# Sums for the last small product on VectorE instead of DMAs, earlier loads and evenly spread splits, in a short convolution layer on one core

## The chip, the core and the metric

The kernel runs on one core of a Trainium2 chip. A core has engines that run on their own and wait for one another through semaphores: TensorE (PE in the profile; PEld is its weight loading) multiplies matrices into eight PSUM banks, VectorE (DVE), ScalarE (ACT) and GpSimd (POOL) work elementwise, and SyncE (SP) issues DMAs, which 16 DMA engines carry out. Each engine takes its own instructions in program order. POOL issues DMAs too, among them the accumulating ones, which add a source to what lies in DRAM. SP's DMAs and POOL's are told apart in the profile as queues q1 and q0.

The metric is the device time of one execution in microseconds. The time before is 778.96 us, the median of three runs (778.84 to 780.01).

## What is computed

With one layer (DEPTH = 1), only the short convolution mixer runs. All arrays are float32: 1024 positions, model width 1024, inner width CI = 2048.

```python
u = rms_norm(x, pre_norm)                              # (1024, 1024)
z, bg, cg, v = jnp.split(u @ w_in, 4, axis=-1)         # w_in: (1024, 4 * 2048)
y = bg * causal_dwconv(cg * v, conv_w) * jax.nn.silu(z)   # 3 taps, (1024, 2048)
m = y @ w_out                                          # w_out: (2048, 1024)
out = x + rms_norm(m, post_norm)
```

## The kernel before

**Matmuls.** A float32 operand is split into a high and a low part: ACT writes the high part (`hi`, rounded to PE's float32 type), and DVE writes the low part (`src - hi`). One product is then three matmuls: low by high, high by low, high by high. Such a pair, hi and lo, is called a piece here, and making it a split.

**First stage.** After the normalisation, `u @ w_in` is computed for 64 groups of 128 columns: four groups plainly, the other 60 in 20 triples of groups, each triple with 20 smaller products by a scheme that saves multiplications (line 931 on). Each triple has 20 steps `s`; behind each step's matmuls the program places reads of the banks, convolution, gates, splits of the next weights and DMAs, by hand. The gated results y go to DRAM as they come (`y_half`, L383): SP stores them into `y_d` and into sums `s_d` for the last stage, and POOL's accumulating DMAs (`more`, L371) finish these sums. Sums of blocks of w_out are made the same way in `t_d`.

**Last stage.** `y @ w_out` is done by products named a, d, b, c, e, f, g in this order (`OUT`, L853), again with sums of blocks as operands. Products a, b, c, e, g are large: two halves h, each 48 matmuls of 512 columns in four banks. Products d and f are small ones, done by seven products p in the order `FP = (1, 2, 6, 5, 7, 3, 4)`, each 24 matmuls of 256 columns (`small_mm`, L1003). Each small product needs one operand of w_out (u) and one of y (y), each of 512 KB. Operands 5, 6, 7 of both sides, 4 of u and 3 of y are sums of blocks. They are made in DRAM: `small_u` (L428) and `small_y` (L442) copy four blocks and then add to the copies with four accumulating DMAs. For d this happens during the triples, with the copies on SP's queue. For f's y the calls stand behind the halves of b and c (`SMALL_Y`, L1113 and L1131), and both copies and accumulates go out on POOL's queue.

**Order of the operands.** `PIECES` (L854) lists the 68 pieces in the order in which they are split, `FETCH` the loads. `fetch_unit` (L869) issues the next load on SP's queue: u's and the small operands into the six buffers of the pool `raw`, the large y operands (1 MB) into the pool `up`, whose 18 buffers also hold the pieces. `split_unit` (L898) makes the next piece: ACT's `hi` (L910, or L907 with the sign turned), DVE's `lo` (L911 or L908). `refill` (L894) issues loads as long as they are no more than five pieces ahead of the splits for small operands, two for large ones. The last triple (`t == END`) issues the first six loads, at the step s = 14 of the triple before and at its own steps 2, 8, 13, 15, 17 (L965), and splits eight pieces (L967). Behind the triples SP's program has the stores of the last gated tiles (L398, L399), then the load of `gpost` (L978), then the loads of `refill`.

**Around the products.** The loop at L1114 emits, for each half or small product, its matmuls and then a number of splits (`SPLITS`, L1110). What empties the banks stands between them: `combine` (L1094) for large products, and for small ones an ACT copy or a DVE sum per product (L1023 to L1029). A bank is used by several small products: 1, 6, 7 and 4 share one, 5 and 3 another. The third product of the order, 6, therefore waits until ACT or DVE has read product 1's result; 7 waits for 6's reading, 3 for 5's and 4 for 7's. These reads stand in ACT's and DVE's order among the splits. In the last lines each row block is normalised and stored (`finish_o`, L1058).

Of the kernel before, what the change touches and what calls it, by code (L numbers as in the profile page):

```python
# [8 lines left out]
F32 = mybir.dt.float32  # L9
# [11 lines left out]
def kernel(  # L21
# [11 lines left out]
    nc = tc.nc  # L33
    P = 128
    _, L, D = x.shape
# [31 lines left out]
    def flat(t):  # L67
        return t.rearrange("p a b -> p (a b)")
# [9 lines left out]
    s_d = dram.tile([P, 4, CH, HB], F32, tag="s_d", name="s_d")  # L78
    t_d = dram.tile([P, 4, CH, HB], F32, tag="t_d", name="t_d")
    SMALLS = "df"  # L80
    sm_y = {i: dram.tile([P, 4, CQ, FC], F32, tag=f"s{i}_d", name=f"s{i}_d") for i in SMALLS}
    sm_u = {i: dram.tile([P, 4, CQ, FC], F32, tag=f"t{i}_d", name=f"t{i}_d") for i in SMALLS}

    def rstd_start(ss, name, n=1):
# [37 lines left out]
    def new_u(name):  # L122
        return up.tile([P, 2, 2, HB], F32R, tag="u", name=name)
# [301 lines left out]
    def block_y(i, a, b):  # L425
        return quarter(s_d[:, SK[i]], b, a)

    def small_u(i, step, ks=slice(0, CQ)):  # L428
        t1, t2, t3, t4 = (sm_u[i][:, n, ks] for n in range(4))
        w11, w12, w21, w22 = (block_u(i, a, b)[:, ks] for a in (0, 1) for b in (0, 1))  # L430
        if step == 0:
            for dst, src in ((t1, w11), (t2, w11), (t3, w22), (t4, w21)):
                nc.sync.dma_start(dst, src)
        elif step == 1:
            more(t1, w12)
            more(t3, w12)
        elif step == 2:
            more(t2, t3)
        else:
            more(t4, t2)  # L440

    def small_y(i, step, ks=slice(0, CQ), queue=None):  # L442
        s1, s2, s3, s4 = (sm_y[i][:, n, ks] for n in range(4))
        y11, y12, y21, y22 = (block_y(i, a, b)[:, ks] for a in (0, 1) for b in (0, 1))
        if step == 0:
            for dst, src in ((s1, y21), (s2, y11), (s3, y21), (s4, y12)):
                (queue or nc.sync).dma_start(dst, src)
        elif step == 1:
            more(s1, y22)
            more(s3, y11)  # L450
        elif step == 2:
            more(s2, s1)
        else:
            more(s4, s2)
# [397 lines left out]
    FP = (1, 2, 6, 5, 7, 3, 4)  # L852
    OUT = [(i, h) for i in "adbcefg" for h in (FP if i in SMALLS else (0, 1))]  # L853
    PIECES, FETCH = [], []  # L854
    for i, h in OUT:
        for side in "uy":
            FETCH.append((side, i, h))
            PIECES += [(side, i, h, q) for q in ((0,) if i in SMALLS else (0, 1))]
    fetched, OP = [], {}

    def small_of(side, i, p):
        sums, blocks = (sm_u[i], block_u) if side == "u" else (sm_y[i], block_y)
        if p in (5, 6, 7):
            return sums[:, p - 5]
        if p == (4 if side == "u" else 3):
            return sums[:, 3]
        return blocks(i, *({1: (0, 0), 2: (1, 0), 3: (1, 1)} if side == "u" else {1: (0, 0), 2: (0, 1), 4: (1, 1)})[p])

    def fetch_unit():  # L869
        if not FETCH:  # L870
            return
        side, i, h = FETCH.pop(0)
        if i in SMALLS:
            t = raw.tile([P, CQ, FC], F32, tag="raw", name=f"r{side}_{i}{h}")
            nc.sync.dma_start(t, small_of(side, i, h))
            fetched.append(t)
            return
        js = slice(h * CQ, (h + 1) * CQ)
        far = slice(CH + h * CQ, CH + (h + 1) * CQ)
        if side == "u":  # L880
            plain_u = {"a": wov[:, js, :HB], "b": wov[:, far, :HB]}
            src = plain_u[i] if i in plain_u else t_d[:, TK[i], js]
            for q in (0, 1):
                r = raw.tile([P, 2, HB], F32, tag="raw", name=f"r{side}_{i}{h}{q}")
                nc.sync.dma_start(r, src[:, 2 * q : 2 * q + 2])
                fetched.append(r)
        else:
            plain_y = {"a": y_d[:, js, :HB], "b": y_d[:, far, :HB], "g": y_d[:, far, HB:]}
            src = plain_y[i] if i in plain_y else s_d[:, SK[i], js]
            t = up.tile([P, 2, 2, HB], F32, tag="u", name=f"r{side}_{i}{h}")  # L890
            nc.sync.dma_start(t.rearrange("p a b c -> p (a b) c"), src)
            fetched.extend([t[:, 0], t[:, 1]])

    def refill():  # L894
        while FETCH and len(fetched) <= len(OP) + (5 if FETCH[0][1] in SMALLS else 2):
            fetch_unit()

    def split_unit(delayed=False):  # L898
        n = len(OP)
        if n >= len(PIECES):  # L900
            return
        side, i, h, q = PIECES[n]
        t = new_u(f"o{side}_{i}{h}{q}")
        src, hi, lo = flat(fetched[n]), flat(t[:, 0]), flat(t[:, 1])
        turn = h == 6 if i in SMALLS else (i == "c") != (h == 1)
        if side == "u" and turn:
            nc.scalar.mul(hi, src, -1.0)  # L907
            low = lambda: nc.vector.scalar_tensor_tensor(lo, src, -1.0, hi.bitcast(F32), op0=ALU.mult, op1=ALU.subtract)  # L908
        else:
            nc.scalar.copy(hi, src)  # L910
            low = lambda: nc.vector.tensor_sub(lo, src, hi.bitcast(F32))  # L911
        if delayed:
            low_us.append(low)
        else:
            low()
        OP[side, i, h, q] = t
# [14 lines left out]
    for t in range(len(TRIPLES)):  # L931
        for s, i in enumerate(ORDER if t else ORDER_0, 1):
            now[0] += 1
            product(t, i)
            read(t, i)
            run_lows()
            while low_us:
                low_us.pop(0)()
            if t == 0:
                first_chunk(s)  # L940
                if s in LOWS:
                    low_u(LOWS[s][0], kks=LOWS[s][1])
            run_due()
            for unit in (SPLIT if t else SPLIT_0).get(s, ""):
                split_w(t, unit)
            if t == 0 and s in HIGHS:
                high_u(HIGHS[s])
            for unit in (NEXT if t else NEXT_0).get(s, ""):
                split_w(t + 1, unit)
            sums(t + 1, (SUMS if t or s > 15 else SUMS_0).get(s, ()))  # L950
            if s == 14:
                fetch_triple(t + 2)
            if s in (7, 14, 20):
                run_later()
            if 2 <= t < 2 + 2 * CH:
                j = (t - 2) // 2
                if t % 2 == 0 and s == 3:
                    fetch_t(j)
                if t % 2 == 0 and s == 15:
                    add_t(j, 0)  # L960
                if t % 2 == 1 and s in (15, 20):
                    add_t(j, 1 + (s == 20))
            for do, *of_small in EARLY.get((t, s), ()):
                do(*of_small)
            if t == END - 1 and s == 14 or t == END and s in (2, 8, 13, 15, 17):  # L965
                fetch_unit()
            if t == END and s in (6, 9, 11, 13, 15, 17, 19, 20):  # L967
                split_unit(True)
# [138 lines left out]
        else:  # L1107
            norm_square(q + TH, 0)

    SPLITS = {("a", 0): 5, ("a", 1): 5, ("c", 0): 5, ("c", 1): 5, ("e", 0): 6, ("e", 1): 5}  # L1110
    SPLITS.update({(i, p): 2 for i in SMALLS for p in FP})
    SPLITS.update({("d", 3): 1, ("d", 4): 1, ("f", 7): 1, ("f", 3): 0, ("f", 4): 0})
    SMALL_Y = {("b", 0): 0, ("b", 1): 1, ("c", 0): 2, ("c", 1): 3}  # L1113
    for n, (i, h) in enumerate(OUT[:-2]):  # L1114
        if (i, h) == ("f", FP[0]):
            load_res(0)
            load_res(1)
        splits = SPLITS.get((i, h), 4)
        if i in SMALLS:
            small_mm(i, h)  # L1120
        for q in range(1 if i in SMALLS else TH):
            if i not in SMALLS:
                out_mm(i, h, q)
                if h == 1 and q > 0:
                    combine(i, q - 1)
            for z in range(splits if i in SMALLS else (splits + TH - 1 - q) // TH):
                split_unit()
                refill()
        if i not in SMALLS and h == 1:
            combine(i, TH - 1)  # L1130
        if (i, h) in SMALL_Y:  # L1131
            small_y("f", SMALL_Y[i, h], queue=nc.gpsimd)
        if i == "c":
            early_half(2 * h)
            early_half(2 * h + 1)
        if i == "f" and h in FP[:TH]:
            early_half(FP.index(h) + TH)
        if i == "f" and h in (3, 4):
            for q in (0, 1) if h == 3 else (2, 3):
                norm_square(q, 1)  # L1140
                finish_o(q)
        if i == "f" and h == 7:
            for t in range(2, NT):
                load_res(t)
# [33 lines left out]
```

## Time and profile before

| | |
|---|---|
| median of 3 runs | 778.96 us (778.84 to 780.01) |
| the profiled execution, its own time | 777.1 us |
| its span, first to last instruction | 775.3 us |
| mean granted TensorE clock | 0.993 |
| last triple's end, first matmul of a | 606.66 us |
| d's matmuls | 628.42 to 660.32 us |
| f's first matmul | 725.6 us |
| g's first matmul | 746.60 us |

Times inside the profile count from the span's start. In a row of a timeline stand start, duration, engine, line, operation, out<-in by the program's names (buffer numbers left out) and, in brackets, the engine's idle time just before and what released it. `ru_d` and `ry_d` are loaded operands of d, `ou_d` and `oy_d` the pieces made of them, `pd` d's banks, `gx` and `res` what its banks are read into; `sd_d` and `sf_d` are the sums of y for d and f in DRAM. "SPq" is SP issuing a DMA, "DMA a<-b" a transfer on its way.

### The profile page before, as it was taken

To read this page: it belongs to the slowest core of one execution; us is meant where nothing else is said; L and a number is where in the kernel's file an instruction comes from. 1 tells how busy PE (TensorE), PEld (TensorE's weight loads), DVE (VectorE), ACT (ScalarE), POOL (GpSimd) and SP (SyncE) were. 2 spreads that over 40 slices of the span, in tenths; PEclk is the share of its full clock that TensorE was granted. 3 is DMA by queue.
4 is the path that set the end of the run, shared out by engine and by line. 5 is a ranking of instruction groups with operands and counts; after the bars stand their busy time and mean duration, and the time that the engine had idled before them with its cause. 6 is when DMAs were issued, how large, how long until landed. Compare 5 with 4: busy or idle time off the path is not lost.

```text
span 775.3 us, 10514 instructions
## 1 busy us (share of the span) xinstructions
PE 758.3 (98%) x3530; PEld 635.0 (82%) x3530; DVE 509.9 (66%) x774; ACT 467.5 (60%) x897; POOL 496.9 (64%) x604
## 2 busy tenths in 40 slices
PE   9999999999999999999999999999999986999996
PEld 8888888888888888888888888888888876888985
DVE  6898776465657565664655565666567755668887
ACT  8869756556656665655666465647548364546742
POOL 0678978778887977797898988889962321100012
PEclk9999999999999999999999999999999998999999
DMA  9402347459377458466877877795659499994944
GB/s 338 125 1 69 96 113 179 125 113 252 70 195 163 116 146 201 105 164 150 188 179 171 188 159 192 147 248 114 148 110 281 94 362 358 354 324 163 376 168 164
DMA packets 123975, 139.67 MB, mean 180 GB/s; under 512 B 6104, under 2 KB 89360, under 8 KB 123408
## 3 DMA queue, kind: packets, MB, share of 16 engines
q1 hardware_dynamic: 107136, 111.72, 44.2%
q0 software_dynamic: 16768, 27.27, 22.1%
q8 instruction: 28, 0.46, 0.2%
q14 instruction: 27, 0.22, 0.1%
q10 hardware_dynamic: 16, 0.00, 0.0%
HBM read 120.09 MB, written 60.82 MB: 233 GB/s over the span
## 4 chain that ended last, share of the span: by engine, by line
PE 88%; DVE 4%; DMA 4%; issue 1%; ACT 1%; POOL 0%; SPq 0%; DVEq 0%; ACTq 0%
PE pX L136 8%; PE pX L137 8%; PE pX L138 8%; PE pY L136 7%; PE pY L137 7%; PE pY L138 7%; PE pV L137 4%; PE pV L138 4%; PE pV L136 4%; PE pW L137 2%; PE pZ L137 2%; PE pW L138 2%; PE pZ L138 2%; PE pW L136 2%; PE pZ L136 2%; DMA ry_b<-y_d 2%
## 5 line engine op out<-in xcount | busy, mean ns | idle before, releaser
L366 DVE TENSOR_TENSOR sn<-sn,pY 128x512 f32<-128x512 f32 x57 | 39.2, 687 | 56.3 <-PE pY L138 26.8
L342 POOL TENSOR_TENSOR g<-g,sn 128x512 f32<-128x512 f32 x29 | 40.2, 1392 | 34.8 <-ACT sn L340 28.3
L366 DVE TENSOR_TENSOR sn<-sn,pX 128x512 f32<-128x512 f32 x57 | 39.3, 689 | 33.5 <-PE pX L138 33.5
L340 ACT ACTIVATE sn<-sn 128x512 f32<-128x512 f32 x24 | 15.2, 633 | 64.1 <-DVE sn L366 40.1
L1070 POOL TENSOR_TENSOR res<-xr,res 128x512 f32<-128x512 f32 x4 | 6.6, 1648 | 72.2 <-DVE res L1069 72.2
L360 ACT ACTIVATE sn<-pV 128x512 f32<-128x512 f32 x38 | 20.6, 596 | 48.0 <-PE pV L138 48.0
L315 POOL TENSOR_TENSOR g<-sn,g 128x512 f32<-128x512 f32 x23 | 31.0, 1349 | 28.6 <-DVE sn L364 28.6
L358 ACT COPY sn<-pZ 128x512 f32<-128x512 f32 x19 | 11.2, 589 | 46.7 <-PE pZ L138 46.7
L372 POOL DMA_DIRECT2D s_d<-s_d x24 | 22.9, 954 | 20.8 <-DMA s_d<-y_d 14.0
L324 POOL TENSOR_TENSOR g<-g,sn 128x512 f32<-128x512 f32 x20 | 28.3, 1413 | 11.7 <-DVE sn L366 11.3
L182 POOL TENSOR_TENSOR raw<-raw 128x256 f32<-128x256 f32 x40 | 32.3, 919 | 0.0
L187 POOL TENSOR_TENSOR raw<-e,raw 128x256 f32<-128x256 f32 x40 | 31.1, 858 | 1.3
L364 DVE TENSOR_TENSOR g<-pY,g 128x512 f32<-128x512 f32 x15 | 10.4, 692 | 30.7 <-PE pY L138 30.7
L183 POOL TENSOR_TENSOR e<-raw,raw 128x512 f32<-128x512 f32 x20 | 26.2, 1312 | 1.6
L1014 PE MATMUL pd<-ou_d,oy_d 128*128 128x256 f32 x56 | 17.2, 308 | 8.7 <-ACT gx L1023 7.4
L136 PE MATMUL pp<-b,wn 128*128 128x512 f32 x62 | 24.6, 397 | 0.0
L137 PE MATMUL pp<-b,wn 128*128 128x512 f32 x62 | 24.4, 393 | 0.0
L138 PE MATMUL pp<-b,wn 128*128 128x512 f32 x62 | 24.2, 390 | 0.0
L305 DVE SCALAR_TENSOR_TENSOR g<-g,cw,cv 128x512 f32<-128x512 f32 x30 | 22.5, 749 | 1.7
L237 DVE TENSOR_TENSOR wE<-wE,wE 128x512 fp32r<-128x512 f32 x20 | 13.7, 687 | 14.0 <-ACT wE L236 14.0
L305 DVE SCALAR_TENSOR_TENSOR cv<-g,cw,cv 128x512 f32<-128x512 f32 x30 | 22.4, 748 | 0.0
L189 POOL TENSOR_TENSOR e<-raw 128x256 f32<-128x256 f32 x20 | 21.8, 1088 | 0.0
(418 smaller groups left out, 3040.9 us busy)
## 6 DMA issues: line engine op xcount, KB each, us to landing
raw<-in_sc_w_in SPq DMA_DIRECT2D x64, 512.0 KB, 5.3
t_d<-in_sc_w_out SPq DMA_DIRECT2D x32, 256.0 KB, 4.5
s_d<-g SPq DMA_DIRECT2D x29, 256.0 KB, 2.1
s_d<-s_d POOLq DMA_DIRECT2D x24, 256.0 KB, 4.6
y_d<-g SPq DMA_DIRECT2D x23, 256.0 KB, 2.7
t_d<-in_sc_w_out POOLq DMA_DIRECT2D x16, 256.0 KB, 7.8
t_d<-t_d POOLq DMA_DIRECT2D x16, 256.0 KB, 4.7
xr<-in_x SPq DMA_DIRECT2D x8, 512.0 KB, 7.8
```

Source lines behind the costliest of these rows:

```text
L136: nc.tensor.matmul(ps, lo, u[:, 0, kk], start=first, stop=False, skip_group_check=True)
L137: nc.tensor.matmul(ps, hi, u[:, 1, kk], start=False, stop=False, skip_group_check=True)
L138: nc.tensor.matmul(ps, hi, u[:, 0, kk], start=False, stop=last, skip_group_check=True)
L182: 0: lambda: (add(w2[:, 0], w2[:, 0], w2[:, 1]), add(w2[:, 2], w2[:, 1], w2[:, 2])),
L183: 1: lambda: sub(e[:, 0:2], w2[:, 0::2], w0[:, 0::2]),
L187: 5: lambda: (sub(w0[:, 2], e[:, 3], w0[:, 2]), sub(w0[:, 0], e[:, 3], w0[:, 0])),
L305: nc.vector.scalar_tensor_tensor(g if j == TAPS - 1 else ps, g, tap(c, j), ps, op0=ALU.mult, op1=ALU.add)
L315: nc.gpsimd.tensor_mul(g, src, g)
L324: nc.gpsimd.tensor_mul(cv, cv, src)
L342: when([(c, "cv", h), (c, "silu", h)], (c, "z", h), {"cv": 1, "silu": 1}, lambda: nc.gpsimd.tensor_mul(cv_of(c, h), cv_of(c, h), t))
L366: nc.vector.tensor_sub(a, a, ps)
L372: nc.gpsimd.dma_start(dst, src, accum_op=ALU.add)
```

## The change

Four things change in the last stage.

1. The four copies and four accumulating DMAs that made f's sums of y in DRAM are gone, and with them the buffer `sf_d`. SP loads the four blocks of y that f needs ("Y" entries), and DVE adds them in SBUF: sum 5 from two blocks, sum 6 from sum 5 and a block, sum 7 from two blocks, sum 3 from sum 6 and a block. The sums lie in `xr` (5 and 6) and in the third part of `res`, `C22` (3 and 7), both of which are used otherwise only later. Operands 1, 2 and 4 are split from the blocks themselves.
2. f's pieces are ordered anew: first its seven y pieces, with 5 ahead of 6 and 7, then its seven u pieces. Sums 5 and 7 are added at their own split, sum 6 at the split of 5, and sum 3 at the split of 6.
3. The last triple issues two loads more, at its steps 18 and 20: operand 2 of d, of both sides.
4. `SPLITS` gives b 5 and 5 (it was the default, 4 and 4), and e 5 and 4 (it was 6 and 5). The total stays the same.

`fetched` becomes a table by piece number, since loads and pieces no longer come in the same order.

```diff
-    sm_y = {i: dram.tile([P, 4, CQ, FC], F32, tag=f"s{i}_d", name=f"s{i}_d") for i in SMALLS}
+    sm_y = {"d": dram.tile([P, 4, CQ, FC], F32, tag="sd_d", name="sd_d")}
...
-    for i, h in OUT:
-        for side in "uy":
-            FETCH.append((side, i, h))
-            PIECES += [(side, i, h, q) for q in ((0,) if i in SMALLS else (0, 1))]
-    fetched, OP = [], {}
+    for i in "adbcefg":
+        if i == "f":
+            n = len(PIECES)
+            FETCH += [("Y", "f", (0, 0), n), ("Y", "f", (1, 0), n + 1), ("Y", "f", (1, 1), n + 1), ("Y", "f", (0, 1), n + 2)]
+            PIECES += [("y", "f", p, 0) for p in (1, 5, 6, 7, 2, 3, 4)]
+            for p in FP:
+                FETCH.append(("u", "f", p, len(PIECES)))
+                PIECES.append(("u", "f", p, 0))
+            continue
+        for h in FP if i in SMALLS else (0, 1):
+            for side in "uy":
+                FETCH.append((side, i, h, len(PIECES)))
+                PIECES += [(side, i, h, q) for q in ((0,) if i in SMALLS else (0, 1))]
+    fetched, OP, blocks_f = {}, {}, {}
...
-            nc.sync.dma_start(t, small_of(side, i, h))
-            fetched.append(t)
+            nc.sync.dma_start(t, block_y(i, *h) if side == "Y" else small_of(side, i, h))
+            if side == "Y":
+                blocks_f[h] = flat(t)
+            else:
+                fetched[n] = flat(t)
...
-        while FETCH and len(fetched) <= len(OP) + (5 if FETCH[0][1] in SMALLS else 2):
+        while FETCH and FETCH[0][3] <= len(OP) + (5 if FETCH[0][1] in SMALLS else 2):
             fetch_unit()
+
+    sum_f = {}
+
+    def sum_of_f(p):
+        if p not in sum_f:
+            a, b = {
+                5: lambda: (blocks_f[1, 0], blocks_f[1, 1]),
+                6: lambda: (sum_of_f(5)[1], blocks_f[0, 0]),
+                7: lambda: (blocks_f[0, 0], blocks_f[1, 0]),
+                3: lambda: (sum_of_f(6)[1], blocks_f[0, 1]),
+            }[p]()
+            t = new_u(f"oy_f{p}0")
+            sum_f[p] = t, {5: xr[:, 0], 6: xr[:, 1], 3: flat(C22[:, :2]), 7: flat(C22[:, 2:])}[p]
+            nc.vector.tensor_add(sum_f[p][1], a, b)
+        return sum_f[p]
...
-        t = new_u(f"o{side}_{i}{h}{q}")
-        src, hi, lo = flat(fetched[n]), flat(t[:, 0]), flat(t[:, 1])
+        if (side, i) == ("y", "f") and h in (3, 5, 6, 7):
+            t, src = sum_of_f(h)
+            if h in (5, 6):
+                sum_of_f({5: 6, 6: 3}[h])
+        else:
+            t = new_u(f"o{side}_{i}{h}{q}")
+            src = blocks_f[{1: (0, 0), 2: (0, 1), 4: (1, 1)}[h]] if (side, i) == ("y", "f") else fetched.pop(n)
+        hi, lo = flat(t[:, 0]), flat(t[:, 1])
...
-            if t == END - 1 and s == 14 or t == END and s in (2, 8, 13, 15, 17):
+            if t == END - 1 and s == 14 or t == END and s in (2, 8, 13, 15, 17, 18, 20):
                 fetch_unit()
...
-    SPLITS = {("a", 0): 5, ("a", 1): 5, ("c", 0): 5, ("c", 1): 5, ("e", 0): 6, ("e", 1): 5}
+    SPLITS = {("a", 0): 5, ("a", 1): 5, ("b", 0): 5, ("b", 1): 5, ("c", 0): 5, ("c", 1): 5, ("e", 0): 5, ("e", 1): 4}
...
-    SMALL_Y = {("b", 0): 0, ("b", 1): 1, ("c", 0): 2, ("c", 1): 3}
...
-        if (i, h) in SMALL_Y:
-            small_y("f", SMALL_Y[i, h], queue=nc.gpsimd)
```

More of the change, by code (lines that the diff above doesn't have):

```diff
@@ L426, in block_y, with small_u @@
         return quarter(s_d[:, SK[i]], b, a)
-    def small_u(i, step, ks=slice(0, CQ)):
+    def small_u(i, step, ks):
         t1, t2, t3, t4 = (sm_u[i][:, n, ks] for n in range(4))
@@ L440, in small_u, with small_y @@
             more(t4, t2)
-    def small_y(i, step, ks=slice(0, CQ), queue=None):
+    def small_y(i, step, ks):
         s1, s2, s3, s4 = (sm_y[i][:, n, ks] for n in range(4))
@@ L446, in small_y @@
             for dst, src in ((s1, y21), (s2, y11), (s3, y21), (s4, y12)):
-                (queue or nc.sync).dma_start(dst, src)
+                nc.sync.dma_start(dst, src)
         elif step == 1:
@@ L871, in fetch_unit @@
             return
-        side, i, h = FETCH.pop(0)
+        side, i, h, n = FETCH.pop(0)
         if i in SMALLS:
-            t = raw.tile([P, CQ, FC], F32, tag="raw", name=f"r{side}_{i}{h}")
-            nc.sync.dma_start(t, small_of(side, i, h))
-            fetched.append(t)
+            t = raw.tile([P, CQ, FC], F32, tag="raw", name=f"r{side}_{i}{h if side != 'Y' else h[0] * 2 + h[1]}")
+            nc.sync.dma_start(t, block_y(i, *h) if side == "Y" else small_of(side, i, h))
[3 more added lines that the diff above has]
+                fetched[n] = flat(t)
             return
@@ L885, in fetch_unit @@
                 nc.sync.dma_start(r, src[:, 2 * q : 2 * q + 2])
-                fetched.append(r)
+                fetched[n + q] = flat(r)
         else:
@@ L891, in fetch_unit @@
             nc.sync.dma_start(t.rearrange("p a b c -> p (a b) c"), src)
-            fetched.extend([t[:, 0], t[:, 1]])
+            fetched[n], fetched[n + 1] = flat(t[:, 0]), flat(t[:, 1])
     def refill():
-        while FETCH and len(fetched) <= len(OP) + (5 if FETCH[0][1] in SMALLS else 2):
+        while FETCH and FETCH[0][3] <= len(OP) + (5 if FETCH[0][1] in SMALLS else 2):
             fetch_unit()
+    sum_f = {}
[11 more added lines that the diff above has]
+        return sum_f[p]
     def split_unit(delayed=False):
```

## The prediction

> **What bounds the kernel now.** I read the page first, then the stretches of the last stage, then what TensorE (PE) waited for there.
>
> ```profile
> span 775.3 us, 10514 instructions
> PE 758.3 (98%) x3530; PEld 635.0 (82%) x3530; DVE 509.9 (66%) x774; ACT 467.5 (60%) x897; POOL 496.9 (64%) x604
> ```
>
> PE is busy for 98% of the span, so only its 17 us of idle time, or the tail, can be won without taking matmuls away. The stretches show where the idle time lies (columns: busy time of PE, PEld, DVE, ACT, POOL; granted clock; DMA share; GB/s):
>
> ```profile
> core 0: us, PE busy (x) PEld busy (x) DVE busy (x) ACT busy (x) POOL busy (x), PEclk, DMA share, GB/s
> 630.00:640.00 10.00, 7.40 (x62) 7.19 (x61) 7.82 (x7) 9.04 (x12) 3.13 (x4) 1.00 1.06 366
> 640.00:650.00 10.00, 6.08 (x49) 5.67 (x47) 4.41 (x5) 3.09 (x4) 1.15 (x2) 0.94 1.05 373
> 650.00:660.00 10.00, 7.79 (x46) 7.58 (x47) 6.90 (x7) 5.05 (x6) 0.89 (x1) 0.72 1.10 342
> 660.00:670.00 10.00, 10.00 (x47) 8.34 (x47) 7.29 (x8) 7.45 (x8) 2.13 (x2) 1.00 1.06 389
> ```
>
> From 630 to 660 PE loses 8.7 us, the DMA engines are full, and the clock falls to 0.72 behind the longest pause. What PE waited for from 616 us on (us in total, times, longest):
>
> ```profile
> PE pd L1014 <- ACT gx L1023: 7.4, 2, 4.8
> PE pd L1014 <- DVE gx L1027: 1.1, 1, 1.1
> PE pf L1014 <- DVE res L1027: 0.4, 1, 0.4
> PE pd L1014 <- ACT gx L1025: 0.2, 1, 0.2
> ```
>
> All but 0.4 us is product d. PE's timeline gives its size (the starts of d's first and second small product, and of b):
>
> ```profile
> 628.42 0.28 PE L1014 MATMUL pd<-ou_d,oy_d 128*128 128x256 f32 x1
> ...
> 631.29 0.28 PE L1014 MATMUL pd<-ou_d,oy_d 128*128 128x256 f32 x1
> ...
> 660.32 0.40 PE L996 MATMUL po_b<-ou_b,oy_b 128*128 128x512 f32 x1
> ```
>
> A small product takes 631.29 - 628.42 = 2.87 us, so d's seven need 20.1 us. They took 660.32 - 628.42 = 31.9: **11.8 us are lost in d**, pauses and slow clock together. That is the most this change can win there.
>
> Why ACT and DVE are late is in the chain that ended last (start, us, what):
>
> ```profile
> 617.58 7.11 DMA ry_d<-s_d
> 624.76 1.06 ACT oy_d L910
> 625.85 1.24 DVE oy_d L911
> 627.11 7.68 DMA ry_d<-sd_d
> ...
> 635.95 1.24 DVE oy_d L911
> ...
> 637.63 15.60 DMA ry_b<-y_d
> 653.25 1.05 ACT oy_b L910
> ...
> 656.69 0.61 DVE gx L1027
> ```
>
> PE waits for an emptied bank; the copy or sum that empties it (L1023, L1027) stands in ACT's and DVE's order behind splits, and the splits wait for loads. The loads go round through six raw buffers: load, split, next load, about 9.5 us a round (617.58 to 627.11). The last link is ry_b, 1 MB, 15.6 us on its way. From its landing at 653.23 to b's start at 660.32 are 7.1 us of splits, bank reading and one small product, so b starts 7.1 us after ry_b lands, or when d's matmuls are through, whichever is later. SP issued nothing for 19 us before that:
>
> ```profile
> 595.54 0.36 SPq L875 DMA_DIRECT2D ry_d<-s_d  x1
> 615.12 0.33 SPq L398 DMA_DIRECT2D s_d<-g  x1
> ```
>
> It stood at the store of the last gated tile. And POOL's queue, which has nothing else to do, sends f's sums of y into the same stretch:
>
> ```profile
> 635.72 2.50 POOL L447 DMA_DIRECT2D sf_d<-s_d  x3
> 645.82 0.75 POOL L447 DMA_DIRECT2D sf_d<-s_d  x1 [7.59 <-issue]
> 649.60 1.29 POOL L372 DMA_DIRECT2D sf_d<-s_d  x1 [3.04 <-issue]
> ```
>
> In the program they stand behind b's halves, but POOL waits only for their data, so they collide with the loads of d and b. The DMA queues (packets, MB, share of the 16 engines) for 617 to 636 us, and then for 636 to 654:
>
> ```profile
> q1 hardware_dynamic: 2894, 5.96, 89.5%
> ```
>
> ```profile
> q1 hardware_dynamic: 2386, 4.47, 67.0%
> q0 software_dynamic: 720, 2.36, 37.4%
> ```
>
> q1 carries SP's transfers, q0 POOL's. In the second stretch q0 takes 0.374 x 18.0 = 6.7 us of the engines' time. A megabyte of q1 costs 0.895 x 19.0 / 5.96 = 2.85 us in the first and 0.67 x 18.0 / 4.47 = 2.70 us in the second.
>
> **The change part by part.**
>
> *f's sums off the DMA queues.* Four copies and four accumulates of 512 KB go, and SP loads four blocks for f where it loaded seven operands. POOL's accumulates of s_d stay:
>
> ```profile
> s_d<-s_d POOLq DMA_DIRECT2D x24, 256.0 KB, 4.6
> ```
>
> One of them, 0.26 of the 2.36 MB, goes out in 636 to 654 (POOL's last, just before its three copies), so 6.7 x 2.10 / 2.36 = 6.0 us of engine time come free ahead of ry_b's landing. The ends: nothing, if the loads wait for raw buffers and not for the engines; all 6.7 if the accumulate costs little. I take 6.0, since the engines stand at 1.05 of full and 15.6 us for 1 MB is no buffer's wait: ry_b was issued long before. What goes after 654 us is hidden, as PE is full from 660.
>
> The Trainium skill, page "DMA: Bandwidth & Descriptors", section "Anatomy of one DMA", prices a GpSimd transfer at 2.0 us plus its bytes by 436 GB/s; by that the 2.10 MB hold the engines for 4.8 us and the next item's 1 MB for 2.4, and the sum below would be an estimate of 7.2, not 8.7. The row, 6.7 us for 2.36 MB, is dearer per byte than the page.
>
> *Two more operands of d in the last triple.* ru_d2 and ry_d2 are issued at the triple's steps 18 and 20, ahead of the store at which SP stood, with raw buffers free (a's first pieces are split by then). So 1 MB leaves the queue that starts at 617: 2.7 us by q1's price. SP issues two DMAs more while it had nothing to do: no cost. The wait goes to ru_d6, two operands further on. The ends: 0, if the buffers alone limit, and 3.2 us, a third of a 9.5 us round for two of six buffers. I take 2.7.
>
> *What is late next.* Sum: ry_b lands 6.0 + 2.7 = 8.7 us earlier, near 644.5, and b starts 8.7 us earlier, as this stays below the 11.8 us at which d's matmuls would set it. A second count agrees: d7's operands are now issued at about 618 to 620 instead of near 627, are split near 632 to 633, ry_b's issue follows near 633.5, and the 2 MB ahead of it with its own 1 MB, at 2.7 us each, end at 641.6 if nothing else is in the way. Of the 11.8 us some 3 stay, before d's last product, which waits for the bank that L1027 empties behind b's first low halves.
>
> *Four additions on DVE.* They fall in c's second half; c, e and f slide forward with b. Their kind is the low half of a split, and two such in a row and DVE's later stretches read:
>
> ```profile
> 707.00 1.23 DVE L911 TENSOR_TENSOR ou_f<-ru_f,ou_f 128x1024 fp32r<-128x1024 f32 x1 [0.19 <-ACT ou_f L910]
> 708.14 1.22 DVE L911 TENSOR_TENSOR oy_f<-ry_f,oy_f 128x1024 fp32r<-128x1024 f32 x1
> ```
>
> ```profile
> 697.00:718.20 21.20, 21.20 (x95) 17.54 (x95) 16.69 (x19) 13.78 (x20) 0.00 (x0) 1.00 0.51 173
> 730.00:740.00 10.00, 10.00 (x85) 9.97 (x84) 10.00 (x16) 7.51 (x12) 0.00 (x0) 1.00 0.95 371
> ```
>
> One costs 1.14 us of DVE's time, four 4.6. The even spread (b 5 and 5, e 5 and 4) puts two splits ahead of c's second half, so that 697 to 718 holds two instructions more than before: 2.3 us. The sum for operand 7 is made just when it is needed, so its low half waits for ACT's copy, about 1.1 us. That is 3.4 us against 21.20 - 16.69 = 4.5 us of idle DVE. I cost it at **nothing**: that idle time hides it. Without the cover it costs one for one, because in f, from 730 to 740, DVE is full (10.00 of 10.00) and PE reads its banks again only when DVE has emptied them. The added waits: ACT's copies of the sums wait for DVE, and behind them stand c's reads of its banks, which nothing on PE needs before g. The sums lie in buffers (xr, C22) whose next writers come half a product later. Raw buffers are held longer by the four blocks; f's u operands behind them are still asked for five pieces ahead of their splits. Nothing.
>
> *Sum.* 8.7 us off a span of 775.3 gives 766.6, and off the profiled execution's own 777.1 us, 768.4. The median shown, 778.96, lies 1.9 us above that execution; the same gain makes it **770.3 us**.
>
> **The rivals.**
>
> *Less relief.* If the buffers' round and not the engines set the pace, only the earlier issue helps, or part of q0's time goes to loads that are not yet needed, since SP issues c's right behind b's. Gain 2.7 to 6: 773 to 776.3. For it: the chain goes through splits as well as loads. Against: ry_b's 15.6 us. 0.20.
>
> *All of it.* If the two queues shared evenly while both had work, q0 cost up to half of 636 to 654, 9.0 us; with 2.7 that is 11.7, d's matmuls set b's start, and the time is about 767. The rows speak against: 37.4% against 67.0%. The Trainium skill, same page, section "Queues, rings and completion order", states such a turn by turn sharing. 0.14.
>
> *DVE keeps f.* The additions cost more than the idle time, and f's start is 1 to 4 us late: 771.3 to 774.3. Against it: 3.4 against 4.5 us. 0.06.
>
> *Slower.* The blocks come too late. DVE goes in order, so an addition that waits for its block holds every split behind it, all of e's and f's. It needs them near 697 - 8.7 = 688 us. The first 4.5 us are idle time, each further one is lost, and from 13.2 us late on the gain is eaten. A load that goes out only when needed, at ry_b's 15.6 us, would cost 2.4 us: 781. Against it: the blocks are asked for half a product before they are needed, and the DMA share near there is 0.51. 0.04.
>
> *Nothing.* The waits in d move to another load with no gain: 777.4 to 780.5. 0.04.
>
> **How the numbers follow.** The forecast, 768.8 to 773, has 0.52. The range goes from all of d's loss won and f's 0.4 us too, 766.6, to the earlier issue alone, 776.3; it leaves out the last two cases. A measurement here can tell about 0.2%, 1.6 us, from no change. Faster by more: 0.52 + 0.20 + 0.14 + 0.06 = 0.92. Within: 0.04. Slower: 0.04.
>
> **What would show it.** Right: ru_d2 and ry_d2 issued near 596 to 606 us; no sf_d transfer; q0's share in 636 to 654 near 5%; ry_b on its way for 9 to 11 us and landed near 644.5; b's first matmul near 651.6; no clock below 0.9 there; PE full from b to f. Wrong: ry_b landing after 650 (less relief); a pause of PE above 1 us in f (DVE); DVE waiting for a block load in c.

## The result, and the profile after

The changed kernel takes **771.16 us** (median of 4 runs, 770.88 to 771.81), the kernel before in the same comparison 778.9 us. The ratio is 0.9904 with a 95% interval of 0.9885 to 0.9922: faster by 7.7 us, where 8.7 were forecast (770.3 us). Compared once more beside the last experiments, it took 770.06 us against 778.67, 0.9892 (0.9878 to 0.9905). The forecast lies between the two medians. What the profiles show of the 1.1 us between them comes below.

The profiled execution is the slowest of the first four, 771.81 us. The head of its page, two of its stretches (columns as before: busy time of PE, PEld, DVE, ACT, POOL; granted clock; DMA share; GB/s), and then what PE waited for from 616 us on (us in total, times, longest). The changed file's lines are L1047 to L1049 for `small_mm` (L1014 to L1016 before), L1029 for `out_mm` (L996), L1056 and L1060 for the copy and the sum out of d's banks (L1023, L1027), L943 and L944 for the two halves of a split (L910, L911), L922 for the new additions:

```profile
span 769.9 us, 10498 instructions
PE 757.7 (98%) x3530; PEld 633.9 (82%) x3530; DVE 513.3 (67%) x778; ACT 466.2 (61%) x897; POOL 489.3 (64%) x596
```

```profile
640.00:650.00 10.00, 6.83 (x55) 6.42 (x54) 6.01 (x7) 6.47 (x7) 0.00 (x0) 1.00 1.06 386
650.00:660.00 10.00, 10.00 (x49) 8.93 (x49) 7.99 (x8) 6.86 (x8) 0.00 (x0) 0.83 1.02 423
```

```profile
PE pd L1047 <- DVE gx L1060: 1.9, 1, 1.9
PE pd L1047 <- ACT gx L1056: 1.2, 1, 1.2
PE pf L1047 <- DVE res L1060: 0.4, 1, 0.4
```

PE's waits in d have shrunk from 8.7 us to 3.1. The DMA engines are as full as before; but the queues of 636 to 654 us show other freight (packets, MB, share of 16 engines):

```profile
q1 hardware_dynamic: 2988, 6.84, 97.1%
q0 software_dynamic: 144, 0.26, 7.9%
```

SP's loads move 6.84 MB where they moved 4.47, and POOL's queue falls from 2.36 MB to 0.26. SP issues the two added operands of d at 596.50 and 597.27, 18 us ahead of the store at which it stands:

```profile
596.50 0.46 SPq L884 DMA_DIRECT2D ru_d<-t_d  x1
597.27 0.36 SPq L884 DMA_DIRECT2D ry_d<-s_d  x1
```

The chain of waits from ry_b to d's last small product, and below it PE's timeline of that product and of b's start:

```profile
634.60 11.09 DMA ry_b<-y_d
...
645.71 1.05 ACT oy_b L943
...
646.79 0.99 DVE oy_b L944
...
647.93 0.80 DVE oy_b L944
...
649.07 0.70 DVE gx L1060
```

```profile
649.80 0.39 PE L1047 MATMUL pd<-ou_d,oy_d 128*128 128x256 f32 x1 [1.95 <-DVE gx L1060]
...
651.10 0.28 PE L1048 MATMUL pd<-ou_d,oy_d 128*128 128x256 f32 x1
651.22 0.36 PE L1049 MATMUL pd<-ou_d,oy_d 128*128 128x256 f32 x1
651.39 0.42 PE L1047 MATMUL pd<-ou_d,oy_d 128*128 128x256 f32 x1
651.60 0.42 PE L1048 MATMUL pd<-ou_d,oy_d 128*128 128x256 f32 x1
...
653.95 0.63 PE L1029 MATMUL po_b<-ou_b,oy_b 128*128 128x512 f32 x1
```

ry_b lands at 645.69 (653.23 before). The order on DVE is the old one: two low halves of oy_b, and behind them the sum `gx` that empties the bank of d's last product. New is what the matmuls' starts show. Up to 651.10 they follow 0.12 us apart; from 651.39 on, 0.21. The clock has fallen (0.83 in the stretch from 650 to 660), 1.6 us after PE took up work again, and d's last product takes 653.95 - 649.80 = 4.15 us in place of 2.87.

In the kernel before, the same slow clock stood one product earlier:

```profile
651.08 0.58 PE L1014 MATMUL pd<-ou_d,oy_d 128*128 128x256 f32 x1 [4.80 <-ACT gx L1023]
651.46 0.42 PE L1015 MATMUL pd<-ou_d,oy_d 128*128 128x256 f32 x1
651.68 0.42 PE L1016 MATMUL pd<-ou_d,oy_d 128*128 128x256 f32 x1
...
657.35 0.39 PE L1014 MATMUL pd<-ou_d,oy_d 128*128 128x256 f32 x1 [1.13 <-DVE gx L1027]
```

There the slow product was followed by another 1.13 us of waiting for DVE, so its slowness cost nothing; the last product ran from 657.35 to 660.32, its matmuls 0.12 us apart again. That is why the slow matmuls, which went on to 655.5, added nothing to the 7.1 us from ry_b's landing to b's start.

### The profile page after: what moved, and what is told of

Read it like the earlier page. It is cut to its first block, busy times and chain, and to the rows that moved or that the text cites. A ratio compares the mean times of both kernels' runs of the same rounds, so it can differ in the third digit from the quotient of the medians.

```text
span 769.9 us, 10498 instructions
## 1 busy us (share of the span) xinstructions
PE 757.7 (98%) x3530; PEld 633.9 (82%) x3530; DVE 513.3 (67%) x778; ACT 466.2 (61%) x897; POOL 489.3 (64%) x596
## 4 chain that ended last, share of the span: by engine, by line
PE 94%; DMA 2%; DVE 2%; issue 1%; ACT 0%; SPq 0%; DVEq 0%
PE pX L136 8%; PE pX L138 8%; PE pX L137 8%; PE pY L136 7%; PE pY L138 7%; PE pY L137 7%; PE pV L138 4%; PE pV L137 4%; PE pV L136 4%; PE po_x L1031 3%; PE po_x L1029 3%; PE po_x L1030 3%; PE pW L138 2%; PE pZ L138 2%; PE pW L136 2%; PE pZ L136 2%
## 5 line engine op out<-in xcount | busy, mean ns | idle before, releaser
L340 ACT ACTIVATE sn<-sn 128x512 f32<-128x512 f32 x24 | 15.2, 631 | 64.1 <-DVE sn L366 40.1
L237 DVE TENSOR_TENSOR wC<-wC,wC 128x512 fp32r<-128x512 f32 x20 | 13.8, 688 | 11.9 <-ACT wC L232 11.9
```

The lines of the kernel that those rows point to most:

```text
L237: lows.append(lambda: nc.vector.tensor_sub(x[:, 1], ps, x[:, 0].bitcast(F32)))
```

## The experiments

Twelve kernels were run in three groups, each group beside the kernel before on one chip. Its medians there are 777.43 us (early operands, sums alone, old spread, copies back on POOL), 778.29 (additions three times, four early, filler, splits behind) and 778.67 (the others). Stage a starts between 606.66 and 607.57 us in the profiles, so events are compared as distances. "To ry_b" is the time from a's first matmul to ACT's first split of ry_b, which starts 0.02 us after the landing; "to b" goes on from there to b's first matmul.

| kernel | median us | ratio to before (95%) | to ry_b | to b |
|---|---|---|---|---|
| before | 777.4 to 778.9 | 1 | 46.6 | 7.07 |
| changed | 771.16 | 0.9904 (0.9885 to 0.9922) | 38.5 | 8.24 |
| changed, again | 770.06 | 0.9892 (0.9878 to 0.9905) | 37.7 | 7.08 |
| early operands alone | 775.69 | 0.9976 (0.9966 to 0.9986) | 42.7 | 9.38 |
| sums on DVE without early operands | 772.02 | 0.9933 (0.992 to 0.9947) | 40.1 | 7.07 |
| changed, old spread of splits | 771.47 | 0.9925 (0.9913 to 0.9938) | 38.0 | 8.37 |
| changed, f's copies back on POOL | 775.89 | 0.9972 (0.9959 to 0.9984) | 43.3 | 8.65 |
| before, f's copies by SP in order | 771.39 | 0.9909 (0.9894 to 0.9924) | 40.3 | 7.08 |
| changed, additions three times | 776.47 | 0.9976 (0.9966 to 0.9986) | 38.6 | 8.32 |
| changed, four operands early | 768.5 | 0.9877 (0.9859 to 0.9895) | 36.6 | 7.07 |
| changed, filler matmuls | 770.03 | 0.9901 (0.9885 to 0.9916) | 38.0 | 7.07 |
| before, b's splits behind | 772.85 | 0.9932 (0.992 to 0.9945) | 46.8 | 2.36 |
| changed, b's splits behind | 766.23 | 0.9849 (0.9834 to 0.9864) | 37.8 | 4.17 |
| the same, four operands early | 766.57 | 0.9847 (0.9834 to 0.9861) | 36.7 | 5.18 |

### Which part of the change wins what

Early operands alone, on the kernel before:

```diff
-            if t == END - 1 and s == 14 or t == END and s in (2, 8, 13, 15, 17):
+            if t == END - 1 and s == 14 or t == END and s in (2, 8, 13, 15, 17, 18, 20):
```

> The kernel before with the two further loads of d in the last triple alone; f's sums stay on the DMA queues and the splits as they were. If DMA engine time sets the pace (the prediction): 1 MB leaves the queue ahead of ry_b, ry_b lands 2.7 us earlier, 2 to 3.5 us faster than before. If the round through the raw buffers sets the pace and the copies cost nothing: nearly the whole gain, 6 to 8 us. If the first pause only moves on to the next load: 0 to 1 us.

Its ry_b, from the chain of waits, and the first matmul of d's last product:

```profile
633.89 15.49 DMA ry_b<-y_d
```

```profile
653.50 0.58 PE L1014 MATMUL pd<-ou_d,oy_d 128*128 128x256 f32 x1 [6.50 <-DVE gx L1027]
653.88 0.41 PE L1015 MATMUL pd<-ou_d,oy_d 128*128 128x256 f32 x1
654.09 0.41 PE L1016 MATMUL pd<-ou_d,oy_d 128*128 128x256 f32 x1
```

ry_b lands 3.9 us earlier (46.6 to 42.7), because it is issued 3.7 us earlier; its way is as long as before. But the kernel gains only 1.7 us, less than the 2 to 3.5 expected. One pause of 6.5 us now stands right ahead of d's last product, the clock has fallen behind it, and b starts 9.4 us after the landing, not 7.1. The slow clock takes back 2.3 us of the 3.9 that the load won.

The sums on DVE alone: the changed kernel, with that line as it was before.

> The change without the two further loads in the last triple. By the prediction q0 leaves 6.0 us of engine time ahead of ry_b: 4.5 to 6.5 us faster than before. By the rival that the buffers' round sets the pace: 0 to 2 us faster.

```profile
638.32 9.15 DMA ry_b<-y_d
```

The row is the chain of waits again: the way of ry_b falls from 15.6 us to 9.15, and it lands 6.5 us earlier. The kernel gains 5.4 us.

The even spread of the splits: the changed kernel with `SPLITS` as before.

> The change with the splits spread as before (b 4 and 4, e 6 and 5). DVE then has four additions, 4.6 us, and 1.1 us of waiting for ACT more between c's second half and f, against 4.5 us of idle time: 0 to 1.5 us slower than the change. If the even spread is what hides the additions: 2 to 4 us slower. If it makes no difference: within 0.5 us.

It is within 0.3 us of the changed kernel's first median. By the ratios to the kernel before it is 0.2 to 0.3% behind (0.9925 against 0.9904 and 0.9892), and its interval lies just above that of the second comparison. But its profile puts that ahead of b, where the clock fell here too (8.37 us). From b's first matmul to the end of the span, where the spread could show, it takes 115.6 us, and the changed kernel 116.0 in the first profile and 115.6 in the second. So the spread is worth nothing that shows.

### Is it the copies' traffic?

The changed kernel, with f's eight transfers put back on POOL's queue at their old places. Nothing reads what they write; DVE's sums stay.

```diff
+        if (i, h) in SMALL_Y:
+            small_y("f", SMALL_Y[i, h], queue=nc.gpsimd)
```

> The change, and beside it the four copies and four accumulates of f's sums on POOL's queue as before; nobody reads their result. If it is their traffic that delayed ry_b (the prediction), the time goes back by 4.5 to 6.5 us, to that of the two further loads alone, and ry_b lands near 651. If something else of the change helped (fewer loads of f, the order of the pieces), it stays within 1.5 us of the change.

ry_b in the chain of waits, and POOL's queue in 636 to 654 us:

```profile
635.00 15.63 DMA ry_b<-y_d
```

```profile
q0 software_dynamic: 720, 2.36, 38.5%
```

The transfers alone bring back the 15.6 us of ry_b and take away all but 1.5 us of the gain. So it is their traffic that cost, not the operands that f loaded from the sums.

The opposite: the kernel before, with all its sums in DRAM, whose copies for f are issued by SP.

```diff
-            small_y("f", SMALL_Y[i, h], queue=nc.gpsimd)
+            small_y("f", SMALL_Y[i, h])
```

> The kernel before, only f's eight copies and accumulates of y sums issued by SP at their place in the program (behind b's and c's halves) in place of POOL's queue, which ran ahead. Nothing is left out. My theory (they cost because they go out in 636 to 654 us, beside the loads of d and b; what goes out once PE is full is hidden): q0's share in that stretch falls from 37% to some 8%, ry_b lands 5 to 7 us earlier, as in the run of the sums alone: 4 to 6.5 us faster than before. Rival (the bytes cost wherever they go, or they hold SP's queue, so that loads of c, e and f behind them come late): no more than 1.6 us faster, or slower, with pauses of PE in b to f.

The edit moves only the four copies, not all eight transfers as the expectation has it; the four accumulates stay on POOL's queue, but wait there for the copies. SP's row for the copies, POOL's queue in 636 to 654, and b's start:

```profile
650.49 7.72 SPq L447 DMA_DIRECT2D sf_d<-s_d  x4
```

```profile
q0 software_dynamic: 144, 0.26, 7.9%
```

```profile
654.09 0.40 PE L996 MATMUL po_b<-ou_b,oy_b 128*128 128x512 f32 x1
```

Behind all loads of b and c in SP's order, the copies go out from 650.49 on, when ry_b has landed (at 646.99), and from b on PE waits no more than f's 0.4 us. It is 7.3 us faster than the kernel before by the medians, above the 4 to 6.5 expected, and b starts 6.3 us earlier by the distance from a. The bytes are the same; the time at which they go out is what cost. This one-word edit reaches 771.39 us, level with the whole change in its first comparison and 1.3 us behind it on the same chip, without an instruction more on DVE.

### The additions on DVE

```diff
-            nc.vector.tensor_add(sum_f[p][1], a, b)
+            for _ in range(3):
+                nc.vector.tensor_add(sum_f[p][1], a, b)
```

> The changed kernel with each of its four additions on DVE issued three times (the second and third write the same sum again). Eight additions more at 1.14 us are 9.1 us of DVE ahead of f. My theory (four additions lie in DVE's idle time of c's second half, and only what exceeds it holds f): in the changed kernel's trace DVE's idle time between the additions and f's first emptied bank adds up to some 4.8 us, so 9.1 - 4.8 = 4.3 us should show: 3 to 6 us slower than the changed kernel's 771.2, near 775.5, and a pause of PE above 1 us in f ended by DVE. Rival one (DVE has far more room there): no slower than 0.8 us. Rival two (an addition holds the path from the first one on, so the change's own four cost 4.6 us): 8 to 10 us slower, near 780.

The same places on DVE's timeline: the changed kernel first, then this one, whose lines stand one further on, with the PE row of f's longest pause and PE's waits for DVE in f:

```profile
691.14 1.22 DVE L922 TENSOR_TENSOR xr<-rY_f,rY_f 128x1024 f32<-128x1024 f32 x1
...
700.47 1.22 DVE L944 TENSOR_TENSOR oy_f<-res,oy_f 128x1024 fp32r<-128x1024 f32 x1 [1.11 <-ACT oy_f L943]
...
712.29 0.69 DVE L1138 TENSOR_TENSOR res<-po_v,res 128x512 f32<-128x512 f32 x1 [1.86 <-ACT res L1137]
...
722.70 0.69 DVE L1060 TENSOR_TENSOR res<-pf,res 128x512 f32<-128x512 f32 x1 [0.97 <-PE pf L1049]
```

```profile
691.29 3.73 DVE L923 TENSOR_TENSOR xr<-rY_f,rY_f 128x1024 f32<-128x1024 f32 x3
...
728.77 0.68 DVE L1061 TENSOR_TENSOR res<-pf,res 128x512 f32<-128x512 f32 x1
```

```profile
729.59 0.36 PE L1048 MATMUL pf<-ou_f,oy_f 128*128 128x256 f32 x1 [2.26 <-DVE res L1061]
```

```profile
PE pf L1048 <- DVE res L1061: 2.9, 3, 2.3
PE pf L1048 <- DVE res L1139: 1.4, 1, 1.4
```

In the changed kernel DVE still waits 0.97 us for PE at f's first sum (L1060), as long as in the kernel before: the four additions are hidden. With eight more, this wait is gone, PE waits 4.3 us for DVE in f where it waited 0.4, and the kernel is 5.3 us slower than the changed one's first median. In the profile, the way from b's first matmul to the end is 5.9 us longer: 3.9 are these waits, and the granted clock of 0.95 over the 33 us from 712 to 745 is about another 1.6. So of 9.1 us some 5 were still free: the cover is real, and it is not wide.

### How much is left ahead of b

Two more operands of d fetched early, on the changed kernel:

```diff
                 fetch_unit()
+            if t == END and s == 20:
+                fetch_unit()
+                fetch_unit()
```

> The changed kernel with two more operands of d fetched at the last triple's step 20, four in all: another 1 MB leaves the queue that starts at 617 us. My theory (the transfers' volume ahead of ry_b sets its landing, 2.7 us a megabyte): ry_b lands 2 to 3 us earlier, near 643; PE's pauses in d shrink below 1.5 us and the clock dip behind them with it: 2 to 4 us faster than the changed kernel, 767 to 769. Rival (the round through six raw buffers sets the pace by now): ry_b's landing moves by less than 1 us, within 0.8 us of the changed kernel.

768.5 us, 1.6 to 2.7 better than the changed kernel's two medians, though the intervals of the ratios overlap (its four runs go from 767.0 to 770.1). ry_b comes 1.1 to 1.9 us earlier, less than the 2.7 of a megabyte. Its issue is 2.2 us earlier by the distance from a, but its way, 11.46 us, is longer than in the changed kernel, so the second megabyte wins less than the first.

Filler matmuls ahead of d's last product:

```diff
+        if (i, p) == ("d", 4):
+            ob["b", 0] = bank("po_b0")
+            spare = OP["y", "d", 3, 0][:, 0, 0, :P], OP["u", "d", 3, 0][:, 0, 0, :FC]
+            for _ in range(15):
+                nc.tensor.matmul(ob["b", 0][:, :FC], *spare, start=True, stop=True, skip_group_check=True)
```

> The changed kernel with 15 matmuls of 256 columns (1.8 us at full clock) added on PE just ahead of d's last small product, into the bank that b's first product then starts afresh: their result is not used. They need nothing that is late and fill the pause of 1.95 us. My theory (the pause brings the slow clock that stretches d's last product from 2.87 to 4.15 us and b's start by 0.4 us): the 24 matmuls of the last product start 0.12 us apart, b starts some 7.1 us after ry_b lands instead of 8.3, and the kernel is 1.2 to 1.7 us faster than the changed one although PE has more to do: near 769.7. Rival (the clock falls for another reason, the load on the chip, or the filler delays the product): no faster, spacing of 0.2 us again, 771 to 773.

PE's timeline (five lines are added, so the lines of `small_mm` are L1052 on; L1046 is the filler):

```profile
646.76 1.96 PE L1046 MATMUL po_b<-ou_d,oy_d 128*128 128x256 f32 x15
649.63 0.39 PE L1052 MATMUL pd<-ou_d,oy_d 128*128 128x256 f32 x1 [0.91 <-DVE gx L1065]
...
652.60 0.40 PE L1029 MATMUL po_b<-ou_b,oy_b 128*128 128x512 f32 x1
```

The pause is down to 0.91 us, the last product takes 2.97 us, and b starts 7.07 us after the landing. The median is 1.1 us below the changed kernel's first one. But the changed kernel, run again in the last group, did the same without filler.

> The changed kernel once more, for a comparison on one chip with the others of this call: 770.5 to 772, and again a pause of 1.5 to 2.5 us ahead of d's last small product. Whether the clock falls behind it is open, as the pause alone may not decide it.

Its stretch 646 to 654 us, with the same stretch of the first profile ahead of it, and PE's rows of the second:

```profile
646.00:654.00 8.00, 6.05 (x41) 5.85 (x40) 6.96 (x7) 4.65 (x5) 0.00 (x0) 0.83 1.04 421
```

```profile
646.00:654.00 8.00, 5.37 (x38) 4.83 (x37) 7.05 (x8) 5.67 (x8) 0.00 (x0) 1.00 1.04 421
```

```profile
649.16 0.39 PE L1047 MATMUL pd<-ou_d,oy_d 128*128 128x256 f32 x1 [2.63 <-DVE gx L1060]
...
652.14 0.40 PE L1029 MATMUL po_b<-ou_b,oy_b 128*128 128x512 f32 x1
```

The pause is even longer, 2.63 us, yet the clock holds at 1.00, and b starts 7.08 us after the landing. So the filler's gain isn't shown to be the filler's. The slow clock behind such a pause comes in some executions and not in others; where it falls on d's last product it costs from 1.2 us (the first profile) to 2.3 us (the early operands alone).

### The order of the splits

Both kernels, with the four splits of b's first half moved behind d's small product 7:

```diff
-    SPLITS.update({("d", 3): 1, ("d", 4): 1, ("f", 7): 1, ("f", 3): 0, ("f", 4): 0})
+    SPLITS.update({("d", 6): 0, ("d", 5): 0, ("d", 7): 6, ("d", 3): 1, ("d", 4): 1, ("f", 7): 1, ("f", 3): 0, ("f", 4): 0})
```

On the changed kernel:

> The changed kernel, only the program's order of splits in d changed: the four splits of b's first half that stood behind d's third and fourth small product (6 and 5) come behind the fifth (7), so that the bank copies and sums of 5 and 7 stand ahead of them on ACT and DVE. My theory (PE's last product of d waits for ry_b only because the sum that empties its bank stands in DVE's order behind ry_b's splits): both pauses in d go (1.2 and 1.9 us), with them the slow clock (1.7 us); d takes 20 to 21 us and b starts near 649 to 650 instead of 654: 4 to 5 us faster than the changed kernel, 766 to 767.5. Rival (b waits for ry_b itself and its splits whatever stands before, or the later splits let go of the raw buffers so late that c's loads are late): less than 1.5 us faster, with a pause of PE ahead of b or c.

What PE waited for from 616 us on is a single row, and DVE's timeline has the sum ahead of the splits:

```profile
PE pf L1047 <- DVE res L1060: 0.4, 1, 0.4
```

```profile
643.23 0.69 DVE L1060 TENSOR_TENSOR gx<-pd,gx 128x512 f32<-128x512 f32 x1 [3.52 <-PE pd L1049]
643.84 2.35 DVE L944 TENSOR_TENSOR ou_b<-ru_b,ou_b 128x1024 fp32r<-128x1024 f32 x2
646.10 2.35 DVE L944 TENSOR_TENSOR oy_b<-ry_b,oy_b 128x1024 fp32r<-128x1024 f32 x2
```

Both pauses are gone. d runs from 628.56 to b's start at 648.72, 20.2 us against an ideal of 20.1. At **766.23 us** this kernel beats both, by 12.1 us the one before.

With four operands of d fetched early as well:

> The changed kernel with both: four operands of d fetched early and b's splits behind small product 7. My theory (in the run with the splits behind alone PE has no pause left from 606 us to f's 0.4 us, so d's own 20.1 us set b's start and earlier loads win nothing): within 0.8 us of that run, 766.2. Rival (what the two won on their own, 2.7 and 4.9 us, adds up): near 763.6.

766.57 us: nothing more. d's own matmuls set b's start now, as the 11.8 us of the prediction had it as the limit.

On the kernel before, without any of the change:

> The kernel before, with nothing of the change, only its splits of b's first half in d put behind small product 7, as in the run on the changed kernel. My theory (in the kernel before b starts 7.1 us after ry_b lands because d's last product stands behind ry_b's splits; without that, b starts two to three us after the landing, when its first operand is split): ry_b still lands near 653, PE pauses once, 3 to 7 us ahead of b, b starts near 655.5 to 656.5 instead of 660.3, less up to 0.6 us of slow clock after the pause: 3.5 to 5 us faster than before. Rival (ry_b lands later by what its splits, and so the raw buffers, wait, or the pause ahead of b costs in slow clock what the order wins): no more than 1.6 us faster.

```profile
655.93 0.50 PE L996 MATMUL po_b<-ou_b,oy_b 128*128 128x512 f32 x1 [2.94 <-DVE oy_b L911]
```

ry_b lands as late as ever, but b starts 2.36 us behind it, on PE's timeline right after the first low half of oy_b. The gain is 4.2 us by the two profiled spans, as expected, and 5.8 by the medians, above it; the profiled execution of the kernel before took 777.1 us, 1.6 less than the median here. By the distance from a, b starts 4.5 us earlier, where the changed kernel's two profiles have 6.9 and 8.9. So half or more of what the change won could be had by moving four splits, with every DMA as it was.

## Why the prediction was right, and where it was off

**What bounds the kernel.** Right. d's loss, ry_b as the last link and the copies beside it are shown from both sides: take the copies away or put them later and ry_b's way falls from 15.6 us to 9 to 11; put them back and it is 15.6 again.

**ry_b 8.7 us earlier (6.0 from the copies, 2.7 from the early operands).** Right in sum: 8.1 us in the first profile, 8.9 in the second. The terms were sized less well, and that their sum fits so closely is in part luck. Alone they measured 6.5 and 3.9; each on top of the other, 4.7 to 5.5 for the copies (copies back on POOL against the changed kernel's two profiles) and 1.6 to 2.4 for the operands. The chain of waits shows how they work. The early operands bring ry_b's issue forward, by 3.5 to 3.8 us with the copies or without. The copies leave its issue where it was (31.0 us behind a's start with them, 30.9 without) and lengthen its way. With both changes the way is 11.09 or 10.37 us and not 9.15, so part of the earlier issue is lost again. Whether the shorter queue or the round of the raw buffers sets the issue is not shown: 3.5 to 3.8 is above the 2.7 of a megabyte and above the 3.2 that the prediction had as the upper end. In the prediction's second count the issue, near 633.5, was right (634.60); its 8.1 us for the way was short. The rival of less relief is out by these numbers, and so is the rival of all of it: the 4.7 to 6.5 us of the copies lie about the row's 6.0, not near the 9.0 of an even share.

**b starts 7.1 us after ry_b.** This is the step that was off, by its size. The 7.1 us came from a stretch whose slow matmuls lay off its path, and the prediction took it over as a constant and wrote "no clock below 0.9". But with ry_b earlier, the pause behind which the clock can fall stands directly ahead of d's last product, where nothing hides the slow matmuls. The stretch measured 7.07 to 7.08 us in six profiles, that of before among them, and 8.24 to 9.38 in the five where the clock fell. In the first profile, b's start was forecast for 651.6 and came at 653.95, 2.3 us later: 0.5 because a began later (607.19 against 606.66, a difference that is there by 45 us, in a part that the change does not touch: the last weight load of L518 starts at 44.1 and 44.6 us), 0.6 because ry_b did, counted from there, and 1.2 by the slow clock. b's own first matmuls lost about another 0.4 to it, and so the last store is issued only 6.0 us earlier; the span ends 5.4 us earlier, as that store also took 0.6 us longer to its end. The medians lie 7.7 us apart, since the profiled execution before took 1.8 us less than its median, and the one after 0.65 us more than its own. The two last stores:

```profile
772.21 0.41 SPq L1045 DMA_DIRECT2D out<-gx  x1
```

```profile
766.23 0.41 SPq L1078 DMA_DIRECT2D out<-gx  x1
```

In the second profile (clock 1.00, 7.08 us) nothing of this is left: b starts at 652.14, 8.9 us earlier by the distance from a, and the median of that comparison is 8.6 us below the kernel before, against 8.7 forecast. So the mechanism was right, and the missing microsecond of the first comparison is where the profile shows a slow clock. That the clock explains the difference of the two medians is the reading of one profile of each, not a test by itself: the filler run does not decide it. The clock recorded for each run agrees with it: 0.994 to 0.997 in the four of the first comparison, 0.997 to 0.998 in those of the second, and 0.002 of 770 us is 1.5 us.

**Some 3 us stay in d.** Right: pauses of 1.22 and 1.95 us, 2.63 in the second profile. That they need not stay was not seen: the prediction took DVE's order, sum behind splits, as given.

**DVE's additions cost nothing.** Right: the 0.97 us of idle time at f's first sum are unchanged, the wait of 1.1 us for ACT is there (the row at 700.47), and tripling the additions measured some 5 us of room behind the four. That is more than the 1.1 us that 4.5 less 3.4 left: the prediction's idle time was that of 697 to 718 alone, and the additions start at 691. The even spread of the splits was costed at nothing, and the run without it shows nothing from b on. The rivals of DVE keeping f and of blocks that come late are out with it, since PE's one wait from b to the end is f's 0.4 us.

**What would show it.** The issues at 596 to 606 us, ry_b's 9 to 11 us under way (11.09 and 10.37) and the share of q0 (7.9%, near 5 forecast) were right; ry_b's landing (645.69 and 645.06, 644.5 forecast) and b's start (653.95 and 652.14, 651.6 forecast) were late; "no clock below 0.9" was wrong in one of two profiles. The lower end of the range is 0.2 us off its own sum: 778.96 less 11.8 and 0.4 is 766.8, not 766.6.

## What to carry to other kernels

Ask of each queue not only how many bytes it moves, but what it moves them beside: transfers that nobody needs yet, on a queue with no other work, run ahead into the stretch where the loads are late, and putting them behind those loads in an ordered queue may win as much as taking them away. When a chain runs from a load through an engine's order to a bank, look for work in that order that doesn't need the load; four splits moved behind the bank's copy and sum won 3.8 to 4.9 us on top of the change. And when a stretch of the old profile is used as a constant, see whether its clock will be the same once the pause has moved.

## What was not expected of the hardware

**Short pauses can bring the slow clock.** In the first profile two pauses, 1.22 and 1.95 us, with one small product of 2.87 us between them, were enough: from 651.39 on d's matmuls start 0.21 us apart, and b's first two still follow 0.43 and 0.38 us apart where the next ones take 0.23. The length of a pause alone does not decide it: single pauses of 2.40, 2.42, 2.44 and 2.57 us brought the slow clock (copies by SP, before with b's splits behind, old spread, sums alone), and pauses of 2.60, 2.63 and 2.94 us did not (the first pause of the kernel before, the changed kernel's second profile, and b's start with the splits behind on the kernel before). The Trainium skill, page "TensorE: Matmul & The Clock Gate", section "HAM oscillation — how this bites in real kernels", gives as its rule that PE should not idle for longer than some 3.4 us. Read as leave to idle for less, it does not fit here, as the pauses of 1.95 to 2.57 us above, followed by the slow clock, are all shorter. The same page's Part 1 says that the window in which activity is watched runs freely; that would let the same pause count in one execution and not in the next, as seen here, but no run here shows the window.

**POOL's copies in DRAM cost the loads at least their bytes' time.** Without the 2.10 MB of copies and accumulates ry_b lands 6.5 us earlier. The Trainium skill, page "DMA: Bandwidth & Descriptors", section "Anatomy of one DMA", would give 4.8 us as an estimate, where the profile's share of engine time gives 6.0. The copies alone side with the second (6.5 us, and 6.3 for the copies by SP); on top of the early operands, 4.7 to 5.5 us, the runs do not tell the two apart.
